# Second layer's projected inputs: half of them moved from attention to the first feed-forward head

## Chip, cores and metric

One core of a Trainium2 chip runs the whole kernel. The metric is the device time of one execution in microseconds; the kernel before is stated as the median of three runs. The trace is of one profiled execution of its own.

## What is computed

The reference is a small encoder of two layers on 768 tokens (two requests of 512 and 256 tokens), width 1024, all in fp32:

```python
for i in range(DEPTH):                                   # DEPTH = 2
    h = rms_norm(x, norm_mix[i])
    x = x + (window_attention(...) if i % 2 == 0 else short_conv(...))
    h = rms_norm(x, norm_mlp[i])
    x = x + jnp.square(jax.nn.relu(h @ mlp_w_up[i])) @ mlp_w_down[i]     # 1024 -> 4096 -> 1024
    gate = jax.nn.sigmoid(rms_norm(x, norm_ple[i]) @ ple_w_gate[i])
    x = x + (p[i] @ ple_w_proj[i]) * gate                # p[i]: 768 x 256
return rms_norm(x, final_norm)
```

The product `p[1] @ ple_w_proj[1]` does not depend on x. It may be computed at any time before the last line of layer 1, and it is this product of which a half moves.

## The kernel before

Activations lie with features on the 128 partitions and the 768 tokens along the free axis: eight blocks `x(m)` of 128 features. A matmul of one block of weights (128 x 128) covers 384 tokens at a time, or 512 and 256 in the attention. Each fp32 product is made of three matmuls: `split` (L81) writes an operand as a high part (a copy on ACT) and a low part (a subtraction on DVE), and high x high, low x high and high x low are summed in PSUM (`group2` L123, `group` L131). `weight` (L92) fetches a block of weights by DMA (SP's queue) and splits it; so each weight costs ACT about one row and DVE another.

The feed-forward part (`mlp`, L853) has 4 groups of 2 "up" chunks and 2 "down" halves for each layer. An up chunk is done in one of two ways. `up_plain` (L897) makes the product directly, in four rounds of 24 matmuls (96 in all). `up` (L956) uses a scheme of seven products instead of eight (`Weights7`, `product7` L434), 84 matmuls in all; it needs sums of activation blocks and sums of weight blocks. The first chunks of a layer are plain, since the sums of activations are made beside them: `Norm7.combine(m)` (L301) makes them on ACT and DVE in a series of pieces (`q` L303, L304 and L320 to L326, `t` L330 and L336). `PLAIN = 3, 2` (L825) says that three chunks are plain in layer 0 and two in layer 1.

The norm before an up chunk is applied after its product: `sum_squares` (L210) adds squares over partitions by four matmuls with ones (`ss`, L226), `acc_parts` (L205) splits their operand (`ah`, `al`), and `rstd_steps` (L234) makes 1/rms on ACT (a table load, two `ln`, one `y`, one `ln`; L242 to L251) and DVE (L252, L259). In `up_plain`, a first chunk for which 1/rms is unknown does `acc_parts` behind its second round and the sum of squares and `rstd_steps` behind its fourth.

PSUM has eight banks: four named A, two B, two C (L103); a product of 768 tokens takes two. Instructions in `mlp` stand in the order in which the code emits them, on ACT, PE and DVE (a manual schedule, L1082); `weave` (L827) takes steps of several lists in turn. In the attention and in its output projection a scheduler sets the order.

`mixer_attention` (L446) handles four groups of heads. Beside some steps of a group it puts other work (`beside`, L778): `inputs1` (L766) loads and splits p[1] in group 0, and `projected(q)` (L759) makes four blocks each of the projected inputs in group 1. `step` (L486) does one block: 12 matmuls (`mm<-p`), copies to `pjs` (L497) and a DMA to DRAM (L498). Scores are matmuls `S` (L667, L668), followed by DVE's row L669 and exponentials on ACT; `queries` (L579) makes the next queries (`mm<-xs_mix`).

Behind the attention, the output projection's loop goes over the eight blocks in the order `PAIRED`, adds the result to `xa` and squares for the norm; `behind(i)` of `first_chunk` (L834) fetches and splits the first up chunk's weights beside it. `mlp` of layer 0 follows.

Of the kernel before, what the change touches and what calls it, by code (L numbers as in the profile page):

```python
# [11 lines left out]
F32 = mybir.dt.float32  # L12
# [6 lines left out]
P = 128  # L19
# [9 lines left out]
CH = 1024  # L29
# [18 lines left out]
def trunk_kernel(ctx: ExitStack, tc: tile.TileContext, a: dict, out: bass.AP):  # L48
# [40 lines left out]
        nc.sync.dma_start(raw[:, : src.shape[1]], src)  # L89
        return raw  # L90

    def weight(src, n, raw=None):  # L92

        m = CH if src is None else src.shape[1]
        if raw is None:
            raw = fetch(src)
        hi = wp.tile([P, CH], F32R, name="whi", bufs=2)
        lo = wp.tile([P, CH], F32R, name="wlo", bufs=2)
        split(hi[:, :m], lo[:, :m], raw[:, :m])
        return blocks(hi[:, :m], n), blocks(lo[:, :m], n)  # L100

# [344 lines left out]
    def mixer_attention():  # L446
# [36 lines left out]
                yield ps[:, :n], o, o + n  # L483
                o += n

        def step(i, w, part, tag, vector):  # L486

            l, m = i // KB, i % KB
            if tag == "L":
                t = ap.tile([P, T], F32, tag="L", name="pjs", bufs=BL)  # L490
            else:
                t = big("pjs")
            for ps, o, e in products(terms_of(w, part, col=m % 4 * P)):
                if vector:
                    dve.tensor_copy(t[:, o:e], ps)
                else:
                    act.activation(t[:, o:e], ps, AF.Copy)  # L497
            nc.sync.dma_start(pj[l][m], t[:])  # L498

        with tc.manual_schedule(engines=order):  # L500
# [31 lines left out]
            w0 = blocks(hi[:], 2), blocks(lo[:], 2)  # L532
            w1 = weight(None, 2, raw=w1)
            for i in range(KB):
                step(i, (w0, w1)[i // 4], part0, "L", i % 2)
# [13 lines left out]
        with s1:  # L549
# [224 lines left out]
            def begin_output():  # L774
# [75 lines left out]

    ET = mybir.EngineType

    def mlp(l, norm, nxt, w, places, early):  # L853


        xs = norm.xs
# [40 lines left out]
        def up_plain(u, w, make, then):  # L897

            nonlocal r

            ps = [both(f"p{i + 1}", {0: "AA", 1: "BC"}.get(u, "AA")[i]) for i in range(2)]
            y1 = y2 = None

            def rects(*which):
# [2 lines left out]


            order = [(0, (0, 6), (0, 1)), (1, (0, 6), (0, 1)), (0, (6, 8), (0, 1)), (1, (6, 8), (0, 1))]
            if u > 0:  # L910
                order = [(i, (0, 8), (o,)) for o in (1, 0) for i in range(2)]
            for n, (i, ks, sides) in enumerate(order):
                for k in range(*ks):
                    m, h = PAIRED[k] % (KB // 2), PAIRED[k] // (KB // 2)
                    c = slice(P * m, P * m + P)
                    hi, lo = w.w[f"w{i + 1}{h + 1}"]
                    for j, (wt, part) in enumerate(((hi, 0), (hi, 1), (lo, 0))):
                        for o in sides:
                            pe.matmul(
                                ps[i][o],  # L920
                                lhsT=wt[:, c],
                                rhs=xs[f"x{h + 1}{1 + o}"][m][part],
                                start=k == 0 and j == 0,
                                stop=k == KB - 1 and j == 2,
                            )
                if n == 0:
                    v = make()
                    split2 = [lambda: v.split("second")] if v.plain else []
                    todo1 = norm.combine(todo.pop(0)) if todo else []
                    rest, pend[:] = pend[:4], pend[4:]  # L930
                    weave(rest, todo1, split2)
                elif n == 1:
                    if r is None:
                        parts = norm.acc_parts()
                    sums = [] if v.plain else [v.sums32, v.sums14, lambda: v.split("direct")]
                    weave(norm.combine(todo.pop(0)) if todo else [], sums, pend)
                    pend.clear()
                elif n == 2:
                    v.split("direct" if v.plain else "s32")
                    if u > 0:  # L940
                        y1, y2 = big("y1"), big("y2")
                        rects((0, 1), (1, 1))
                else:
                    if r is None:
                        steps = norm.rstd_steps(psum, norm.sum_squares(psum, parts=parts, tag="C"))
                        weave(steps, norm.combine(todo.pop(0)) if len(todo) > 1 else [])
                        r = norm.r
                        y1, y2 = big("y1"), big("y2")
                        rects((0, 1), (1, 1))
                    rects((0, 0))  # L950
                    squared(y1)
                    rects((1, 0))
                    pend.extend(acts_of(u, y1, y2, y2))
            return v

        def up(u, w, make, then):  # L956

            w.low("s32")
            w.split("s14")
# [7 lines left out]
            act.activation(c, a, AF.Copy)  # L967
            late()
            w.split("w22")
            late()  # L970
            b = bank("B", "b")[:, :H]
            product7(b, w, "s3", xs, True)
            p = big("p")[:, :H]
            act.activation(p, b, AF.Copy)
# [101 lines left out]
                        add(m, ps[i])  # L1076
                        nxt.block(m, x(m))

        jobs = [(up_plain, 0), (up_plain, 1)]
        for g in range(NG - 1):  # L1080
            jobs += [(up if 2 * g + 2 >= PLAIN[l] else up_plain, 2 * g + 2), (down, g, 0), (down, g, 1), (up, 2 * g + 3)]
# [149 lines left out]

    xs0 = [*range(32, 42), *range(8, 15), *range(16, 20), *range(7)]
    act0 = [7, *range(20, 24), 28, 29, *range(24, 28), 15, 30, 31]

    held = xs0[17:] + act0 + [xs0[16]]
# [2 lines left out]


    n1 = Norm7(2, "mlp0", xs0, act0[7:11], act0[11])
    w0, behind = first_chunk(0, n1, 0)
    w = [weight(a["w_o0"][2], 4), weight(a["w_o2"], 2)]
    for i, m in enumerate(PAIRED):
        if i == 4:
            w[0] = weight(a["w_o0"][3], 4)
        ps = both()
        if m < KB // 2:
            group2(ps, terms_of(w[0], [p[4:] for p in aos], col=m % 2 * P))  # L1250
        else:
            group2(ps, terms_of(w[1], [p[6:] for p in aos], col=(m - 4) * P))
        add(m, ps, xa[m])
        n1.block(m, x(m))
        behind(i)
    n2 = Norm(4, "ple0", xs0[:16], xs0[16])
    mlp(0, n1, n2, w0[0], act0, 0)
    n3 = Norm(1, "mix1", xs0[17:] + act0[:5], act0[5])
    ple(n2, n3, act0[6:9])

# [91 lines left out]
```

## Time and profile before

| | |
|---|---|
| runs | 1717.53, 1717.26, 1715.05 us; median 1717.26 |
| profiled execution | 1715.87 us, its span 1714.1 us |
| busy share of the span | PE 98%, DVE 78%, ACT 50%, POOL 0% |
| matmuls | 9554 |
| DMA | 143.80 MB, mean 84 GB/s |
| attention's end, start of the output projection's loop | 285.2 us |
| loop's end, start of layer 0's chunk 0 | 310.2 us |
| largest single wait of PE in a feed-forward part | 8.0 us, at 344.8 us |

A row of the timeline reads: start, duration, engine, line, operation, output<-inputs, shape, count; in brackets the idle time of the engine ahead of it and who ended it. A row of a wait list reads: engine, its tile and line, what it waited for, then the sum, the number of times and the longest. PE's rows overlap, since matmuls are pipelined; the pace is read from start to start.

### The profile page before, as it was taken

What the parts mean: (1) busy time and instruction counts of PE and PEld (TensorE: products, weight loads), DVE (VectorE), ACT (ScalarE), POOL (GpSimd) and SP (SyncE); (2) the same over time, 40 slices, a digit from 0 to 9 for tenths busy, and PEclk for the clock granted to TensorE, in tenths of its full rate; (3) what the DMA queues carried; (4) which work ended last, traced back from release to release, by engine and by line L of the source; (5) the groups of instructions that cost most, each with busy time, mean ns of one, the idle gap of its engine ahead of it and who ended that gap; (6) DMA issues with size and microseconds to landing.
All of it is one profiled execution on the core that took longest, in us unless ns stands there. A gap on an engine that the chain in (4) does not pass through costs nothing. (4 is left out here: it accounts for less than half of the span.)

```text
span 1714.1 us, 24208 instructions
## 1 busy us (share of the span) xinstructions
PE 1672.0 (98%) x9554; PEld 1616.8 (94%) x9554; DVE 1339.6 (78%) x2198; ACT 855.7 (50%) x1363; POOL 2.0 (0%) x30
## 2 busy tenths in 40 slices
PE   8999999979999999999999999999999999999996
PEld 7887878979999999999999999999999999999986
DVE  7587788878999999977764444667989999999676
ACT  6467756645455455545541111445455555545454
POOL 0000000000000000000000000000000000000000
PEclk9999999989999999999999999999999999999998
DMA  8653331112221222122312121211221222222222
GB/s 263 189 146 110 114 109 62 45 50 74 65 84 62 75 74 74 62 84 93 108 62 62 62 62 62 76 60 49 74 73 64 74 75 74 65 71 86 74 89 96
DMA packets 47554, 143.80 MB, mean 84 GB/s; under 512 B 6048, under 2 KB 10656, under 8 KB 47440
## 3 DMA queue, kind: packets, MB, share of 16 engines
q1 hardware_dynamic: 44880, 139.10, 25.8%
q10 hardware_dynamic: 2560, 3.15, 0.7%
q8 instruction: 75, 1.23, 0.3%
q14 instruction: 39, 0.32, 0.1%
HBM read 122.31 MB, written 10.48 MB: 77 GB/s over the span
## 5 line engine op out<-in xcount | busy, mean ns | idle before, releaser
L83 ACT ACTIVATE whi<-wraw 128x1024 fp32r<-128x1024 f32 (+2 forms) x74 | 76.6, 1035 | 183.9 <-PE b L129 53.2
L409 ACT ACTIVATE whi<-sum 128x1024 fp32r<-128x1024 f32 x55 | 57.9, 1053 | 146.6 <-PE a L441 146.6
L866 ACT ACTIVATE y<-y 128x768 f32<-128x768 f32 x64 | 53.4, 838 | 140.5 <-DVE y L863 140.5
L84 DVE TENSOR_TENSOR wlo<-wraw,whi 128x1024 fp32r<-128x1024 f32 (+2 forms) x74 | 88.2, 1191 | 11.7 <-ACT whi L83 11.4
L441 PE MATMUL a<-act,whi 128*128 128x384 f32 x448 | 96.7, 337 | 0.0
L441 PE MATMUL a<-t,zhi 128*128 128x384 f32 x440 | 90.7, 337 | 1.8 <-ACT c L967 1.8
L441 PE MATMUL b<-t,zhi 128*128 128x384 f32 x440 | 90.5, 337 | 0.9 <-DVE y L863 0.9
L441 PE MATMUL a<-t,whi 128*128 128x384 f32 x440 | 90.5, 337 | 0.0
L1023 DVE TENSOR_TENSOR x<-x,a 128x384 f32<-128x384 f32 x112 | 60.8, 553 | 35.1 <-PE a L441 34.8
L441 PE MATMUL a<-xs,whi 128*128 128x384 f32 x432 | 84.5, 337 | 0.0
L138 PE MATMUL mm<-xs_mix,whi 128*128 128x512 f32 (+1 forms) x320 | 83.3, 342 | 0.0
L441 PEld LDWEIGHTS a<-t,zhi 128*128 128x128 f32 x440 | 77.9, 188 | 2.1 <-ACT c L967 2.1
L441 PEld LDWEIGHTS a<-act,whi 128*128 128x128 f32 x448 | 79.8, 188 | 0.0
L441 PEld LDWEIGHTS b<-t,zhi 128*128 128x128 f32 x440 | 77.7, 188 | 1.2 <-issue 1.2
L441 PEld LDWEIGHTS a<-t,whi 128*128 128x128 f32 x440 | 77.8, 188 | 0.0
L441 PEld LDWEIGHTS a<-xs,whi 128*128 128x128 f32 x432 | 76.3, 188 | 0.0
L420 DVE TENSOR_TENSOR wlo<-wraw,whi 128x1024 fp32r<-128x1024 f32 x60 | 73.0, 1217 | 1.9 <-ACT whi L409 1.9
L420 DVE TENSOR_TENSOR wlo<-sum,whi 128x1024 fp32r<-128x1024 f32 x55 | 67.2, 1222 | 9.2 <-ACT whi L409 9.2
L409 ACT ACTIVATE whi<-wraw 128x1024 fp32r<-128x1024 f32 x60 | 63.2, 1054 | 17.4 <-issue 10.3
L420 DVE TENSOR_TENSOR zlo<-sum,zhi 128x1024 fp32r<-128x1024 f32 x55 | 66.9, 1217 | 1.9 <-ACT zhi L409 1.9
L409 ACT ACTIVATE zhi<-sum 128x1024 fp32r<-128x1024 f32 x55 | 58.3, 1060 | 19.9 <-DVE sum L385 16.1
L330 ACT ACTIVATE t<-y 128x768 fp32r<-128x768 f32 x56 | 47.0, 841 | 40.6 <-DVE y L321 27.9
(279 smaller groups left out, 4647.9 us busy)
## 6 DMA issues: line engine op xcount, KB each, us to landing
wraw<-in_up SPq DMA_DIRECT2D x64, 512.0 KB, 3.5
wraw<-in_down SPq DMA_DIRECT2D x64, 512.0 KB, 3.5
wraw<-in_w_in SPq DMA_DIRECT2D x24, 512.0 KB, 3.4
wraw<-in_gate SPq DMA_DIRECT2D x16, 512.0 KB, 3.5
pj<-pjs SPq DMA_DIRECT2D x16, 384.0 KB, 2.9
wraw<-in_w_q SPq DMA_DIRECT2D x8, 512.0 KB, 4.9
wraw<-in_w_out SPq DMA_DIRECT2D x8, 512.0 KB, 3.4
x_in<-in_x SPq DMA_DIRECT2D x8, 384.0 KB, 7.2
```

What stands on the lines that cost most here:

```text
L83: first = act.activation(hi, src, AF.Copy)
L84: dve.tensor_tensor(lo, src, hi.bitcast(F32), ALU.subtract)
L138: pe.matmul(ps[:, o:e], lhsT=w, rhs=x[:, o:e], start=i == 0 and j == 0, stop=i == n - 1 and j == 2,)
L330: act.activation(t[0][:], (self.q1, self.q2)[i][:], AF.Copy)
L409: act.activation(hi[:], src, AF.Copy)
L420: dve.tensor_tensor(lo[:], src, hi[:].bitcast(F32), ALU.subtract)
L441: pe.matmul(ps, lhsT=a, rhs=b, start=start and i == 0, stop=i == len(terms) - 1, skip_group_check=True)
L866: act.activation(t[:], t[:], AF.Square)
L1023: dve.tensor_tensor(t[:, o : o + H], t[:, o : o + H], f, op)
```

## The change

Four things change. In the attention, `projected` makes four blocks instead of eight. The other four are made by `ahead`, at the head of layer 0's feed-forward part, ahead of chunk 0; for this `second_inputs` loads and splits p[1] and the weights again beside the output projection's loop, where it takes the place of `first_chunk`. In layer 0, two chunks instead of three are plain, so chunk 2 is made by `up`. And the sum of squares and `rstd_steps` stand earlier: in layer 0 in `ahead`, behind the four products; in layer 1 behind chunk 0's second and third rounds. Besides, the first `up` of each layer takes other banks for `c` and `b` and another order of pending work, and `w_o2` lies in other buffers.

```diff
-            def projected(q):
-                w = weight(a["proj"][1, q], 2)
-                for i in range(4):
-                    step(KB + 4 * q + i, w, part1, "t", False)
+            def projected():
+                w = weight(a["proj"][1, 0], 2)
+                for m in range(KB // 2):
+                    step(1, m, w, part1, "t", False)
...
-                (1, 5): (lambda: projected(0), lambda: projected(1)),
+                (1, 5): (projected,),
...
-    PLAIN = 3, 2
+    PLAIN = 2, 2
...
+    def second_inputs(places):
...
+        def behind(i):
+            if i < 2:
+                raw = fetch(a["p"][1, :, i, :])
+                hi, lo = (slot(places[2 * i + p], "p1") for p in range(2))
+                split(hi[:], lo[:], raw[:, :T])
...
+            elif i == 3:
+                ws.append(weight(a["proj"][1, 1], 2))
+            elif i == 5:
+                ws.append(up_chunk(0, 0))
+            elif i == 7:
+                ws[1].split("second")
+
+        def product(m):
+            ps = both("pj", "AB"[m % 2])
+            group2(ps, terms_of(ws[0], part, col=m * P))
+            return ps
...
+    def ahead(norm, product, w, places):
...
+        def copied(m):
+            t = slot(places[m], "pjs", F32)
+            for f, o, e in pieces(ps[m]):
+                act.activation(t[:, o:e], f, AF.Copy)
+            nc.sync.dma_start(pj[1][KB // 2 + m], t[:])
+
+        for m in range(KB // 2):
+            ps.append(product(m))
+            if m == 0:
+                w.split("direct")
+                parts = norm.acc_parts()
+            else:
+                copied(m - 1)
+            if m == 2:
+                weave(norm.combine(0))
+        ss = norm.sum_squares(psum, parts=parts, tag="C")
+        copied(m)
+        weave(norm.rstd_steps(psum, ss), norm.combine(1))
+        return norm.r
...
     def up_plain(u, w, make, then):
...
                 if n == 0:
...
+                    if not known:
+                        parts = norm.acc_parts()
                     weave(rest, todo1, split2)
                 elif n == 1:
-                    if r is None:
-                        parts = norm.acc_parts()
...
+                    if not known:
+                        ss = norm.sum_squares(psum, parts=parts, tag="C")
                 elif n == 2:
-                    v.split("direct" if v.plain else "s32")
+                    weave([lambda: v.split("direct" if v.plain else "s32")], [] if known else norm.rstd_steps(psum, ss))
...
     def up(u, w, make, then):
+            first = u == PLAIN[l]
...
-            late()
-            c = bank("C", "c")[:, :H]
+            if not first:
+                late()
+            c = bank("A" if first else "C", "c")[:, :H]
             act.activation(c, a, AF.Copy)
-            late()
+            late(3 if first else 1)
...
-            b = bank("B", "b")[:, :H]
+            b = bank("A" if first else "B", "b")[:, :H]
...
+            if product:
+                r = ahead(norm, product, w, places[5:7] + places[12:])
+                todo = todo[2:]
...
-    w0, behind = first_chunk(0, n1, 0)
-    w = [weight(a["w_o0"][2], 4), weight(a["w_o2"], 2)]
+    behind, product, w0 = second_inputs(xs0[24:])
+    w = [weight(a["w_o0"][2], 4)] * 2
+    w2 = weight(a["w_o2"], 2, tag="z")
```

On PE, in the attention's second group, these rows stand in before between one S of 384 columns and the next (`mm<-p` are the products that move; four blocks of them follow one another here, with one S pair ahead, and the listing shows the last):

```order
L138 MATMUL mm<-p_1302,whi 128x512
L138 MATMUL mm<-p_1303,whi 128x512
L138 MATMUL mm<-p_1302,wlo 128x512
L138 MATMUL mm<-p_1302,whi 128x256
L138 MATMUL mm<-p_1303,whi 128x256
L138 MATMUL mm<-p_1302,wlo 128x256
L667 MATMUL S<-khh,q 128x384
L668 MATMUL S<-kll,q 128x384
```

And in after at the same place, between the same two S (`mm<-xs_mix` are the next queries; 29 such rows stand there, of which the first and the last are shown):

```order
L666 MATMUL S<-khh,q 128x384
L667 MATMUL S<-kll,q 128x384
L138 MATMUL mm<-xs_mix_166,whi 128x512
L138 MATMUL mm<-xs_mix_165,wlo 128x512
...
L138 MATMUL mm<-xs_mix_186,whi 128x256
L138 MATMUL mm<-xs_mix_187,whi 128x256
L138 MATMUL mm<-xs_mix_186,wlo 128x256
L666 MATMUL S<-khh,q 128x384
L667 MATMUL S<-kll,q 128x384
```

The products are gone, and the next queries, which in before stood among the scores behind, have come forward in their place.

On ACT, at the head of layer 0's feed-forward part, before has this behind the split `ah` of the norm's squares (`zhi` in the sixth row is the high part of chunk 1's weights; `q` and `t` are the pieces of `combine`):

```order
L83 ACTIVATE ah<-acc_mlp_3406 128x768
L303 ACTIVATE q<-x,vec 128x768
L304 ACTIVATE q<-x,vec 128x768
L330 ACTIVATE t_3788<-q 128x768
L330 ACTIVATE t_3793<-q 128x768
L409 ACTIVATE zhi<-wraw 128x1024
L303 ACTIVATE q<-x,vec 128x768
L304 ACTIVATE q<-x,vec 128x768
L242 ACT_TABLE_LOAD
L246 ACTIVATE ln<-ss,eps 128x384 x2
```

After has, from the same row on:

```order
L83 ACTIVATE ah<-acc_mlp_3328 128x768
L887 ACTIVATE pjs<-pj 128x384 x4
L303 ACTIVATE q<-x,vec 128x768
L304 ACTIVATE q<-x,vec 128x768
L330 ACTIVATE t_3678<-q 128x768
L330 ACTIVATE t_3683<-q 128x768
L887 ACTIVATE pjs<-pj 128x384 x4
L303 ACTIVATE q<-x,vec 128x768
L304 ACTIVATE q<-x,vec 128x768
L242 ACT_TABLE_LOAD
L246 ACTIVATE ln<-ss,eps 128x384 x2
```

Eight copies of the new products have come in, and chunk 1's `zhi` is no longer ahead of the norm's rows: it is the fourteenth row behind the last one shown here, with two `ln` and `y` rows, a weight and three more pairs of `t` pieces ahead of it.

More of the change, by code (lines that the diff above doesn't have):

```diff
@@ L90, in fetch, with weight @@
         return raw
[L92 removed]
+    def weight(src, n, raw=None, tag="w"):
         m = CH if src is None else src.shape[1]
@@ L96, in weight @@
             raw = fetch(src)
-        hi = wp.tile([P, CH], F32R, name="whi", bufs=2)
-        lo = wp.tile([P, CH], F32R, name="wlo", bufs=2)
+        pool, bufs = (wp, 2) if tag == "w" else (more, 1)
+        hi, lo = (pool.tile([P, CH], F32R, tag=f"{tag}{p}", name=f"{tag}{p}", bufs=bufs) for p in ("hi", "lo"))
         split(hi[:, :m], lo[:, :m], raw[:, :m])
@@ L943, in up_plain @@
                 else:
[L944 to L947, printed above, removed]
+                    if not known:
                         y1, y2 = big("y1"), big("y2")
@@ L964, in up @@
             product7(a, w, "w11", xs, True)
-            late()
-            c = bank("C", "c")[:, :H]
+            if not first:
+                late()
+            c = bank("A" if first else "C", "c")[:, :H]
             act.activation(c, a, AF.Copy)
-            late()
+            late(3 if first else 1)
             w.split("w22")
             late()
-            b = bank("B", "b")[:, :H]
+            b = bank("A" if first else "B", "b")[:, :H]
             product7(b, w, "s3", xs, True)
```

36 lines of the change are left out of this document (22 added, 14 removed).

## The prediction

> **What bounds the kernel now.** I read the busy times of the page first, then the waits of the matmul engine, then the places where it waits. TensorE is busy nearly the whole span; ACT half of it.
>
> ```profile
> PE 1672.0 (98%) x9554; PEld 1616.8 (94%) x9554; DVE 1339.6 (78%) x2198; ACT 855.7 (50%) x1363; POOL 2.0 (0%) x30
> ```
>
> So a change gains only by removing matmuls, or by removing one of the few stretches in which PE stands still or runs at a lower clock. Windows of 25 us (start and end; then PE busy and its count, PEld, DVE, ACT, POOL, granted clock) show the one large stretch in the part that the change rewrites.
>
> ```profile
> 300.00:325.00 25.00, 25.00 (x145) 25.00 (x144) 24.02 (x36) 17.67 (x23) 0.00 (x0) 1.00 0.16 56
> 325.00:350.00 25.00, 19.78 (x114) 19.45 (x112) 17.43 (x28) 15.12 (x20) 0.00 (x0) 0.99 0.14 43
> 350.00:375.00 25.00, 20.84 (x104) 20.33 (x105) 19.27 (x28) 10.84 (x14) 0.00 (x0) 0.81 0.13 43
> ```
>
> A full window holds 145 matmuls; the two behind it hold 114 and 104. PE's rows in the first feed-forward head of layer 0 show why. Chunk 0 starts at 310.37, the sum of squares at 327.13, chunk 1 behind it ends at 344.8, then comes the hole.
>
> ```profile
> 310.37 0.34 PE L919 MATMUL p<-xs,zhi 128*128 128x384 f32 x1
> ...
> 327.13 0.34 PE L226 MATMUL ss<-ah,ones 128*128 128x384 f32 x1
> ...
> 344.44 0.34 PE L919 MATMUL p<-xs,wlo 128*128 128x384 f32 x1
> 352.79 1.01 PE L919 MATMUL p<-x,zhi 128*128 128x384 f32 x2 [8.01 <-ACT zhi L409]
> 355.17 0.69 PE L919 MATMUL p<-x,zlo 128*128 128x384 f32 x1 [1.37 <-DVE zlo L420]
> 355.66 0.84 PE L919 MATMUL p<-xs,zhi 128*128 128x384 f32 x2
> ```
>
> Chunk 0's 96 matmuls take 16.76 us, 0.1746 us each. Chunk 2 waits 8.01 us for its first weights (zhi, split by ACT), 1.37 us for their low part, and starts at half the pace: after 355.66 two matmuls take 0.64 us. The granted clock agrees.
>
> ```profile
> 356.00:359.00 3.00, 3.00 (x11) 3.00 (x10) 1.41 (x4) 2.45 (x4) 0.00 (x0) 0.50 0.48 175
> 360.00:361.00 1.00, 1.00 (x8) 1.00 (x7) 0.97 (x3) 0.00 (x0) 0.00 (x0) 1.00 0.00 0
> ```
>
> The slow matmuls cost about 2.3 us more (13 between 355.17 and 359.50 take 4.33 us instead of 2.27; the two at 352.79 the rest). ACT's rows say why zhi is late: it is the last of a queue that starts with the norm.
>
> ```profile
> 328.04 0.94 ACT L303 ACTIVATE q<-x,vec 128x768 f32<-128x768 f32 x1 [1.87 <-PE ss L226]
> ...
> 329.82 1.28 ACT L242 ACT_TABLE_LOAD   x1
> 331.12 1.05 ACT L246 ACTIVATE ln<-ss,eps 128x384 f32<-128x384 f32 x2
> ...
> 337.01 0.85 ACT L330 ACTIVATE t<-q 128x768 fp32r<-128x768 f32 x1 [2.34 <-DVE q L326]
> ...
> 351.70 1.04 ACT L409 ACTIVATE zhi<-wraw 128x1024 fp32r<-128x1024 f32 x1
> ```
>
> ACT and DVE hand the pieces of each `combine` to and fro; the hole is a chain between these two engines, not a missing matmul.
>
> **The change, part by part.** All terms are against this execution, 1715.87 us.
>
> *Attention loses four blocks of products.* Here is the stretch that goes (PE, then DVE).
>
> ```profile
> 172.83 0.63 PE L138 MATMUL mm<-p,whi 128*128 128x512 f32 x2
> ...
> 182.07 0.28 PE L138 MATMUL mm<-p,wlo 128*128 128x256 f32 x1
> 182.19 0.34 PE L667 MATMUL S<-khh,q 128*128 128x384 f32 x1
> ```
> ```profile
> 176.59 1.23 DVE L84 TENSOR_TENSOR wlo<-wraw,whi 128x1024 fp32r<-128x1024 f32 x1 [3.75 <-ACT whi L83]
> ...
> 182.75 0.62 DVE L669 CUSTOM_DVE_ANT_0 L<-S,bias,sink 128x384 f32<-128x384 f32 x1 [2.85 <-PE S L668]
> ```
> ```profile
> 172.50:182.75 10.25, 10.20 (x56) 8.71 (x57) 3.14 (x12) 6.74 (x18) 0.00 (x0) 1.00 0.73 266
> 182.75:226.00 43.25, 40.82 (x239) 34.43 (x238) 39.53 (x115) 31.68 (x80) 0.00 (x0) 1.00 0.40 114
> 226.00:285.20 59.20, 58.57 (x350) 50.10 (x349) 49.73 (x143) 36.96 (x93) 0.00 (x0) 1.00 0.17 53
> ```
>
> From 172.83 to 182.19 PE does these products, 9.36 us, with one S pair of 0.34 between them: 9.0 us is the most that can go. But the order of after does not put the next scores (S) there. It puts 29 matmuls of the next queries, 23 of 512 columns and 6 of 256. The products were 24 of each width, so 9.0 us make 0.25 and 0.125 us a matmul and 6.5 us for these 29; and they need their weights split first, on ACT and DVE, as the weights of the products did (wlo ends at 177.8 now). So the next scores come at about 182, as before. Behind that, from 182.75 to 226.00, DVE is busy 39.53 of 43.25 us: PE has 6.5 us less to do there, DVE only one weight split of 1.23 less. At most 3.7 + 1.2 = 4.9 us can go in that stretch; half of its idle time and half of the split would be 2.5. Against this stands that 182 may become 183, as the order puts more ahead of the weight split's low part than now. I take -2.0 us; bounds 0 (DVE sets the pace throughout) and -9.0 (all of it comes through).
>
> *Out-projection loop.* The loop now carries two splits of p, a projection weight and both halves of chunk 0's weights. A low part of p is one DVE row of 128x768 like this one, and one of them stands ahead of the last xa sum, for which PE waits already:
>
> ```profile
> 285.22 0.94 PE L129 MATMUL mm<-aos,whi 128*128 128x384 f32 x4 [0.60 <-DVE xa L736]
> ```
> ```profile
> 325.25 0.96 DVE L336 TENSOR_TENSOR t<-q,t 128x768 fp32r<-128x768 f32 x1
> ```
>
> So the loop starts between 0 and 0.96 us later; +0.3. Inside the loop PE is saturated and DVE has 24.02 of 25 us in the window from 300, part of it chunk work that moves behind the loop, so I cost the rest at nothing; if a split falls between two `add`s, it costs its 1.2 us once. SP gets two fetches of p more, the projection weight later, and four writes of pj among chunk 1's loads. Such a write lands in 2.9 us, and the DMA engines' share in the windows above is 0.16 and less, so these too cost nothing; if a chunk's load were held up by all four, it would land some 12 us later.
>
> ```profile
> pj<-pjs SPq DMA_DIRECT2D x16, 384.0 KB, 2.9
> ```
>
> *The head of layer 0.* Matmuls: 48 of the four products come in, and chunk 2 has 84 instead of 96: +36 x 0.1746 = +6.3 us. The stalls I get by walking the rows of ACT, DVE and PE in the new order, each starting when its engine is free and its inputs are there, with the durations of this trace; the same walk over the old order sets chunk 2's zhi 0.9 us too late, which I take off. The new rows, eight PSUM copies on ACT, have a near relative:
>
> ```profile
> L1018 ACT ACTIVATE B<-a 128x384 f32<-128x384 f32 x56 | 26.9, 481 | 24.7 <-PE a L441 24.7
> ```
>
> Three products run at 310.2 to 316.5. The fourth needs product 1's banks, whose copies stand on ACT behind a zhi and three 128x768 rows (about 3.4 us from 313.1 on by the rows above, and the last, `ah`, waits 1.4 us for DVE's sum): the copies end at 319.5, so PE waits **3.1 us** there (2.4 to 3.1). The sum of squares follows at 321.7, chunk 0 from 322.4 to 339.1. On ACT stand now ahead of chunk 1's zhi the eight copies (3.3 us, as the next one starts before the last has ended), eight q (6.7) and eight t pieces (6.0), the table load (1.3), the `ln` and `y` rows (2.8) and a weight (1.0). The walk's posts are: first q and t pieces done at 323.8, last copies 325.4, table load 328.3, second `ln` 331.1, next t pieces 334.8 (a wait of 2.2 for DVE among them), weight 337.4, t pieces 340.5 (a wait of 1.6), the last ones 344.8. There zhi of chunk 1 starts, less the 0.9 at 343.9. PE therefore waits about **5.8 us** before chunk 1 and **0.9 us** for zlo, then 2.2 us at half clock as now. Chunk 2 finds its weights there. Its end comes at 378.3 - 0.9 + 2.2 = 379.6 against 373.7 now: **+5.9 us**. The other way round: +6.3 of matmuls, while the stalls are 3.1 + 5.8 + 0.9 + 2.2 = 12.0 instead of 8.0 + 1.4 + 2.3 = 11.7. The norm's sums come early, yet its chain still stands behind the new copies, so the hole moves from chunk 2 to chunk 1 and hardly shrinks. Bounds: +3.7 (full clock after the shorter hole) and +8.1 (half clock also behind the fourth product).
>
> After the 8.01 us hole the clock stood at 0.50, while the 1.82 us wait at 1185.62 (below) is followed by a full-rate pace (8 matmuls in 1.67 us): between these two the trace says nothing. [...]
>
> *Layer 1.* Its chunk 2 now writes c and b through bank A and pops the pending work in another order.
>
> ```profile
> 1181.44 1.65 PE L441 MATMUL b<-t,zhi 128*128 128x384 f32 x8 [0.91 <-DVE y L863]
> 1182.93 0.87 PE L441 MATMUL b<-t,zlo 128*128 128x384 f32 x4
> 1185.62 1.67 PE L441 MATMUL a<-t,zhi 128*128 128x384 f32 x8 [1.82 <-ACT c L967]
> ```
>
> Copy c moves ahead of two ACT rows, and up to 0.91 + 1.82 = 2.7 us could go; but DVE's chain, which is unchanged, gives the low part for the next `down` where PE waits already, and takes it back. The norm is summed a round sooner, but ACT's zhi behind it still waits for PE's round 2. I take -0.2; bounds 0 and -2.7.
>
> **Sum:** -2.0 + 0.3 + 5.9 - 0.2 = +4.0, so 1719.9 for this execution. That one is 1.4 us below the median of the runs shown (1717.26), so the forecast at the median's level is **1721.3 us**, +0.23%. A difference under 0.2% (3.4 us) is about what a measurement of this kernel cannot tell from none.
>
> **Rivals.**
>
> *Nearly nothing.* The hole before chunk 1 is 2 us shorter, with the full clock back sooner, or attention gives 4: the sum falls to 0 to +3, some 1717 to 1720.6. For it: every bound above reaches there. Against it: both have to go beyond their nearest rows.
>
> *The hole is filled (faster).* The products' 8.4 us of matmuls stand in the hole's place, so that only issue counts. Then the head costs +6.3 - 8.0 + 3.1 less the slow clock of 2.3, about -0.9, and attention gives 2 to 5: 1711 to 1714. It decides at one point: chunk 1's zhi must start by 339, when chunk 0 ends. For it: sums of squares are out 5.4 us sooner (321.7 against 327.13). Against it: the ACT rows listed above, with the 3.4 us ahead of them, are 24.5 us from 313.1 on; alone they end at 337.6, and any hand-overs of over 1.4 us put zhi past the point. The same result comes from attention alone if its next scores arrive 8 us sooner, against which the order's 29 matmuls speak.
>
> *Twice half clock (slower still).* The clock falls also behind the fourth product's wait, if 3 us are long enough for it, or a smaller PE load in attention leaves gaps as at 158 to 161. That gives +2.2, and with attention at 0 another +2: 1723.5 to 1725.5.
>
> ```profile
> 158.00:161.00 3.00, 2.63 (x10) 2.25 (x11) 2.33 (x7) 0.93 (x3) 0.00 (x0) 0.54 1.04 257
> ```
>
> Here a clock of 0.54 stands beside a PE that is busy for 2.63 of 3 us.
>
> *The change doesn't do what it says* would be that the moved products bring no relief to attention; that is the lower price of 0 above, 1723.3 us.
>
> **How the numbers follow.** Forecast (1719.5 to 1723, moved hole, small attention gain): 0.46. Nearly nothing: 0.22. Filled or full attention gain: 0.14. Slower still: 0.18. Eight times in ten the time lies between 1712 and 1725.5, which takes in half of the faster case and the whole of the slowest. Faster by over 0.2% (below 1713.8): 0.14. Slower by over 0.2% (above 1720.7): 0.18 and 0.36 of the forecast, 0.54 together. Within: 0.22 and the 0.10 of the forecast below 1720.7, 0.32.
>
> **What would show it.** In the changed kernel: a wait of 2.4 to 3.1 us at the fourth `pj` product for the copies of L887; a wait of 5 to 7 us of chunk 1's first matmul for ACT's zhi, with a clock near 0.5 behind it; no wait of over 1 us at chunk 2; 48 more matmuls behind the loop; in attention, scores at 182 and the loop's start about 2 us sooner than 285.2. I am wrong if chunk 1 starts within 2 us of chunk 0's end, if the loop starts 5 us sooner, or if the clock stays at 1.00 throughout the head.

## The result and the profile after

The changed kernel takes 1717.88 us (median of 20 runs, 1715.01 to 1720.30), the kernel before in the same series 1716.99 us (20 runs, 1713.98 to 1719.18). The ratio is 1.0007, with a 95% interval of 1.0000 to 1.0014: +1.2 us, from 0 to +2.4. That is within 0.2%. The forecast was +4.0 us, or 1721.3. The time lies inside its wide range (1712 to 1725.5) but below its main case (1719.5 to 1723), and the outcome held likeliest (slower by over 0.2%) did not come.

The profiled executions differ more: 1720.30 us for after (span 1718.5) against 1715.87 for before. A pair of single executions is thus read with care below: the trace says in which place time goes, the medians say how much in all.

The page's row of busy times of after hardly differs:

```profile
PE 1675.4 (97%) x9542; PEld 1617.8 (94%) x9542; DVE 1346.7 (78%) x2207; ACT 860.1 (50%) x1370; POOL 2.0 (0%) x30
```

Windows of 25 us over the head of layer 0, after:

```profile
300.00:325.00 25.00, 22.72 (x121) 22.21 (x120) 21.87 (x32) 18.39 (x29) 0.00 (x0) 0.93 0.29 96
325.00:350.00 25.00, 19.15 (x99) 18.32 (x98) 18.16 (x27) 17.02 (x22) 0.00 (x0) 0.86 0.17 53
350.00:375.00 25.00, 25.00 (x146) 25.00 (x145) 20.07 (x30) 12.65 (x17) 0.00 (x0) 1.00 0.13 43
```

The empty place has moved: the third window is full now (146 matmuls, 104 before), and the first two have lost 24 and 15. PE's timeline of after shows the two holes:

```profile
308.60 0.86 PE L129 MATMUL pj<-p,whi 128*128 128x384 f32 x4
...
317.35 1.71 PE L129 MATMUL pj<-p,whi 128*128 128x384 f32 x4 [2.28 <-ACT pjs L887]
318.85 0.84 PE L129 MATMUL pj<-p,wlo 128*128 128x384 f32 x2
...
321.25 0.33 PE L226 MATMUL ss<-ah,ones 128*128 128x384 f32 x1
...
344.48 1.01 PE L971 MATMUL p<-x,zhi 128*128 128x384 f32 x2 [5.60 <-ACT zhi L409]
345.74 0.69 PE L971 MATMUL p<-x,zlo 128*128 128x384 f32 x1 [0.25 <-DVE zlo L420]
...
378.12 0.86 PE L441 MATMUL a<-act,whi 128*128 128x384 f32 x4
```

The fourth product waits 2.28 us for the copies of L887, chunk 1 waits 5.60 us for ACT's zhi, and chunk 2 waits for nothing. Behind both waits the clock is at about half, as the granted clock (the third number from the right) of windows over the two places shows:

```profile
317.30:321.20 3.90, 3.85 (x12) 3.66 (x13) 2.34 (x5) 2.87 (x5) 0.00 (x0) 0.56 0.96 297
...
344.40:349.00 4.60, 4.27 (x14) 3.76 (x15) 3.15 (x6) 1.91 (x4) 0.00 (x0) 0.57 0.39 112
349.00:352.00 3.00, 3.00 (x19) 3.00 (x18) 2.61 (x5) 0.91 (x3) 0.00 (x0) 1.00 0.02 8
```

From the first row to `down` the head takes 378.12 - 308.60 = 69.52 us, before 373.72 - 310.37 = 63.35: +6.2 us. From `down` to the end both spans have 1340.4 us left, so layer 1 gave nothing in sum. Its chunk 2 still waits for the copy c, 1.87 us instead of 1.82. The wait of 0.91 us for DVE's `y` ahead of it is gone, but a wait of 0.84 us for another `y` has come behind it:

```profile
1188.76 1.67 PE L441 MATMUL a<-t,zhi 128*128 128x384 f32 x8 [1.87 <-ACT c L1023]
...
1198.26 1.68 PE L441 MATMUL a<-xs,whi 128*128 128x384 f32 x8 [0.84 <-DVE y L1046]
```

**Where the attention's gain shows.** The row of scores ahead of the removed products stands in before and in after at the following times; all PE rows ahead of it are the same in both kernels (first fence before, second after).

```profile
172.49 0.38 PE L667 MATMUL S<-khh,q 128*128 128x256 f32 x1
```
```profile
175.50 0.39 PE L666 MATMUL S<-khh,q 128*128 128x256 f32 x1
175.72 0.28 PE L667 MATMUL S<-kll,q 128*128 128x256 f32 x1
175.84 0.40 PE L138 MATMUL mm<-xs_mix,whi 128*128 128x512 f32 x1
176.07 0.34 PE L666 MATMUL S<-khh,q 128*128 128x384 f32 x1
...
182.49 0.34 PE L666 MATMUL S<-khh,q 128*128 128x384 f32 x1
...
283.45 0.93 PE L129 MATMUL mm<-aos,whi 128*128 128x384 f32 x4 [1.20 <-DVE xa L735]
```

This execution came to the row 3.0 us later than before's, for reasons that lie ahead of the change, and to the output projection's loop 1.8 us sooner (283.45 against 285.22). The part between has therefore lost 4.8 us. The runs below repeat this: 14 traces hold the old or the new attention.

| stretch of PE | old order (5 traces) | new order (8 traces) |
|---|---|---|
| start of the row S 128x256 | 170.2 to 173.4 | 170.2 to 175.5 |
| from it to the second S 128x384 (182.19 in before) | 9.68 to 9.72 | 6.97 to 7.00 |
| from there to the loop's start | 103.0 to 103.7, mean 103.2 | 100.6 to 101.7, mean 101.1 |

The first stretch is 2.7 us shorter, the second 2.1: 4.8 us, with the loop's later start (a wait of 1.20 instead of 0.60 us) already in it. The fourteenth trace is that of the first experiment, e1_attn_half: 172.3, 7.00 and 100.0 us, and its loop starts behind a wait of 0.60 us, as in before.

### The profile page after: what moved, and what is told of

It reads as the page before. It is cut to its first block, busy times and chain, and to the rows that moved or that the text cites. A ratio compares the mean times of both kernels' runs of the same rounds, so it can differ in the third digit from the quotient of the medians.

```text
span 1718.5 us, 24204 instructions
## 1 busy us (share of the span) xinstructions
PE 1675.4 (97%) x9542; PEld 1617.8 (94%) x9542; DVE 1346.7 (78%) x2207; ACT 860.1 (50%) x1370; POOL 2.0 (0%) x30
```

## Experiments

Each was timed in five rounds beside the kernel before on the same chip; the ratio is to that kernel. "Head" is PE's time from the first row behind the output projection's loop to the first `down` row. Two experiments can be told apart when they differ by more than about 2 us.

| kernel | ratio (95%) | us | head, us | PE's waits over 0.4 us in the head |
|---|---|---|---|---|
| before | 1 | 0 | 63.35 | 8.01 zhi, 1.37 zlo |
| after | 1.0007 (1.0000 to 1.0014) | +1.2 | 69.52 | 2.28 copies, 5.60 zhi |
| e1_attn_half | 0.9975 (0.9965 to 0.9985) | -4.3 | 62.66 | 8.01 zhi, 1.38 zlo |
| e2_head_only | 1.0040 (1.0026 to 1.0053) | +6.9 | 70.38 | 2.27 copies, 7.07 zhi |
| e3_plain3 | 1.0019 (1.0010 to 1.0029) | +3.3 | 71.94 | 2.28 copies, 5.53 zhi |
| e4_zhi_early | 0.9991 (0.9983 to 1.0000) | -1.5 | 68.35 | 2.28 copies, 0.50 zlo, 2.63 c |
| e5_copies_first | 0.9986 (0.9977 to 0.9994) | -2.4 | 65.65 | 1.18 zhi, 0.64 zlo, 0.50 zlo, 2.63 c |
| e7_copies_only | 0.9998 (0.9989 to 1.0007) | -0.3 | 69.17 | 8.09 zhi |
| e8_c_first | 0.9987 (0.9978 to 0.9995) | -2.2 | 65.77 | 1.19 zhi, 0.64 zlo, 1.07 d, 1.85 y |
| e10_pool | 1.0001 (0.9992 to 1.0010) | +0.2 | 68.47 | 1.19 zhi, 0.64 zlo, 3.75 whi, 0.66 c, 0.85 y |
| e12_nosums | 0.9979 (0.9971 to 0.9988) | -3.6 | 64.65 | 1.19 zhi, 0.64 zlo, 2.63 c, 0.86 y |
| e6_before_zhi | 0.9990 (0.9982 to 0.9999) | -1.7 | 60.01 | 1.84 zhi, 0.64 zlo, 5.81 y |
| e9_before_zhi_pool | 1.0011 (1.0000 to 1.0021) | +1.9 | 63.58 | 1.83 zhi, 0.64 zlo, 7.87 y |
| e11_before_zhi_nosums | 0.9986 (0.9978 to 0.9995) | -2.4 | 59.47 | 1.83 zhi, 0.64 zlo, 5.28 y |

The us column is the ratio's distance from 1 times 1716. The heads are of one execution each: those of after and e2_head_only, which are the same code, differ by 0.9 us, so a smaller difference says nothing. In the last three kernels the head ends at a wait, and the slow matmuls behind it are not in the column: from `down` to the end they have 1342.1, 1343.8 and 1342.2 us left, all others 1339.7 to 1340.9.

### The two halves apart

Half of the attention's products left out of before, and made nowhere:

```diff
-                (1, 5): (lambda: projected(0), lambda: projected(1)),
+                (1, 5): (lambda: projected(0),),
...
-        nc.sync.dma_start(pr[:, :n], pj[l][m, :, o : o + n])
+        nc.sync.dma_start(pr[:, :n], pj[l][m % 4 if l else m, :, o : o + n])
```

> The kernel before with four of the eight blocks of the second layer's projected inputs left out of the attention, and made nowhere (the last step reads the first four blocks twice). It prices the relief of the attention alone. Theory A (the two traces, aligned row by row around the change: after runs 3.0 us later ahead of the removed products and 1.8 us sooner behind them): -4.8 us, 1712. Theory B (the prediction's term: DVE sets the pace behind): -2.0 us, 1715. If nothing came through: 1717.

-4.3 us, from -6.0 to -2.6: theory A's 4.8 lies inside, the prediction's 2.0 does not. Theory A's figure has the later start of the loop in it, which this kernel doesn't have; without it (0.6) the figure is 5.4 and lies inside as well.

The new head with the old attention:

```diff
-            def projected():
-                w = weight(a["proj"][1, 0], 2)
-                for m in range(KB // 2):
-                    step(1, m, w, part1, "t", False)
+            def projected(q):
+                w = weight(a["proj"][1, q], 2)
+                for i in range(4):
+                    step(1, 4 * q + i, w, part1, "t", False)
...
-                (1, 5): (projected,),
+                (1, 5): (lambda: projected(0), lambda: projected(1)),
```

> The changed kernel, but with all eight blocks still made in the attention as before; four of them are then made a second time in the head, and written over the first. It prices everything except the attention's relief. Theory A: head +6.2, layer 1 nothing, start of the loop +0.6 by the longer wait for the last xa sum: +6 to +7, 1723 to 1724. Theory B (attention gives 2, so that the rest costs 3): 1720.

+6.9 us (4.5 to 9.1), as theory A has it. Of these the head holds 7.0 (70.38 against 63.35); the wait at the loop's start is 1.19 us here and 0.60 in before, which prices that step at +0.6. The two halves sum to +2.6, the change itself measured +1.2; the intervals are wider than the difference. PE's timeline of this kernel also answers how its two holes hang together:

```profile
320.11 1.18 PE L129 MATMUL pj<-p,whi 128*128 128x384 f32 x4 [2.27 <-ACT pjs L887]
...
347.24 1.01 PE L971 MATMUL p<-x,zhi 128*128 128x384 f32 x2 [7.07 <-ACT zhi L409]
```

The fourth product waits as in after (2.27 and 2.28 us), but here the pace hardly drops behind it (12 matmuls in 2.42 us, from 320.11 to 322.53, instead of 3.90). Nothing is won by that: chunk 1 starts 35.88 us behind the head's first row in both kernels, and PE waits 7.07 us ahead of it instead of 5.60. ACT sets this start, whatever PE does before it.

### The third plain chunk

```diff
-    PLAIN = 2, 2
+    PLAIN = 3, 2
```

> The changed kernel with three plain chunks in layer 0, as before: chunk 2 has 96 matmuls again instead of 84. If matmuls alone count: +12 x 0.1746 = +2.1 us on after, 1720. If a hole comes back at chunk 2, since a plain chunk wants its weights sooner: +3 to +6. If the cheaper chunk had brought nothing: 1718.

+3.3 us against before, so +2.1 against after (1.0019 - 1.0007, uncertain by about 2 us), as the 12 matmuls alone give. The head is 2.4 us longer, and chunk 2 has no wait in either trace. So the seven-product chunk is a gain of matmuls and costs no wait in this place.

### Is it the order on ACT that makes the hole?

In after, the split of chunk 1's first weights moved ahead of the last pieces of `combine`:

```diff
                     split2 = [lambda: v.split("second")] if v.plain else []
+                    sooner = known and v.plain
+                    if sooner:
+                        split2.append(lambda: v.split("direct"))
...
-                    weave([lambda: v.split("direct" if v.plain else "s32")], [] if known else norm.rstd_steps(psum, ss))
+                    weave([] if sooner else [lambda: v.split("direct" if v.plain else "s32")], [] if known else norm.rstd_steps(psum, ss))
```

> The changed kernel with the split of chunk 1's first weights (zhi on ACT, zlo on DVE) moved ahead of the last three series of pieces of combine. Theory of the order on ACT: zhi runs at 336.5 instead of 343.4, zlo by 338.4, before chunk 0 ends at 338.9; PE's wait of 5.6 us, 0.25 us and the slow matmuls behind it (2 us) go: -6 to -8 us on after, about 1710.5. Rival: the pieces that are now late make chunk 2 wait, or the buffer of the old weights comes free too late, and under 3 us are won: over 1715.

The hole before chunk 1 is gone: chunk 1 follows chunk 0 without a wait. But only 1.2 us of the head went, and 2.7 us of the time against after (uncertain by about 2), where the theory had 6 to 8: the rival won. PE's timeline of this kernel shows the new place, chunk 2:

```profile
354.24 1.58 PE L441 MATMUL a<-xs,whi 128*128 128x384 f32 x8
355.96 0.97 PE L441 MATMUL a<-xs,wlo 128*128 128x384 f32 x4
356.77 1.57 PE L441 MATMUL b<-t,zhi 128*128 128x384 f32 x8
358.84 0.96 PE L441 MATMUL b<-t,zlo 128*128 128x384 f32 x4 [0.50 <-DVE zlo L420]
362.43 2.93 PE L441 MATMUL a<-t,zhi 128*128 128x384 f32 x8 [2.63 <-ACT c L1026]
```

Counted from the head's first row (307.26 here, 308.60 in after), chunk 2 starts at 46.98 us instead of 54.86, 7.9 us sooner. Then it waits for the copy c, and runs at about half the pace behind it (2.93 us for eight matmuls, 1.57 above). ACT's timeline says that c stands behind a square, which waits 5.19 us for DVE:

```profile
360.21 0.84 ACT L917 ACTIVATE y<-y 128x768 f32<-128x768 f32 x1 [5.19 <-DVE y L914]
360.96 1.04 ACT L409 ACTIVATE whi<-sum 128x1024 fp32r<-128x1024 f32 x1
361.91 0.47 ACT L1026 ACTIVATE c<-a 128x384 f32<-128x384 f32 x1
```

The same edit in the kernel before (with `u > 0` in place of `known`, and an `if not sooner:` ahead of the old split), for its chunk 2:

> The kernel before with nothing changed but the place of chunk 2's zhi and zlo: one series of combine and the pieces of chunk 0's result stand behind them now. Theory of the order on ACT: zhi at 345.5 instead of 351.7, zlo by 347.8; PE's 8.0 + 1.4 us shrink to about 2.9 and the clock stays up: -7 to -9 us, 1708. Rival (the pieces moved back come late for the next half, or the buffer comes free too late): within 3 us of before.

-1.7 us (-3.1 to -0.2) instead of -7 to -9: again the rival. PE's three waits:

```profile
344.43 0.62 PE L919 MATMUL p<-x,zhi 128*128 128x384 f32 x2 [1.84 <-ACT zhi L409]
...
345.69 0.45 PE L919 MATMUL p<-x,zlo 128*128 128x384 f32 x1 [0.64 <-DVE zlo L420]
368.19 1.62 PE L441 MATMUL a<-act,whi 128*128 128x384 f32 x4 [5.81 <-DVE y L863]
```

The hole of 8.01 + 1.37 became 1.84 + 0.64, and a hole of 5.81 us opened at the end of the head, where none was. The head is 3.3 us shorter; 1.7 of it is lost again to the slow matmuls behind the new hole (granted clock 0.56 from 368.1 to 372). What ends the head is thus not the zhi alone; DVE's rectified rows `y` end it too, a few us behind.

### Does removing a wait of PE pay by itself?

The copies of the first two new products moved ahead of `ah` on ACT, first on top of e4_zhi_early, then alone on after:

```diff
             if m == 0:
                 w.split("direct")
-                parts = norm.acc_parts()
             else:
                 copied(m - 1)
             if m == 2:
+                parts = norm.acc_parts()
                 weave(norm.combine(0))
```

> The kernel of e4_zhi_early with the copies of the first two new products moved ahead of the split of the norm's squares (ah) on ACT. The fourth product's wait of 2.3 us and the slow matmuls behind it (1 to 2 us) go in any case. Theory of ACT's queue: ACT's rows up to chunk 1's zhi do not start sooner for it, so that PE waits again ahead of chunk 1 for what it wins: 0 to -1.5 us on e4, 1713 to 1714.5. Rival (waits of PE add up): -3.3 to -4.3 us, 1710 to 1711.

> The changed kernel with only the copies moved ahead of ah. The wait of 2.3 us at the fourth product goes. Theory of ACT's queue: the wait ahead of chunk 1 grows by as much, within 1 us of after (1717). Rival (waits add up): -2.3 to -4 us, 1713 to 1715.

In the second the wait of 2.28 us at the fourth product is gone, and PE's timeline shows where most of it went:

```profile
340.19 1.01 PE L971 MATMUL p<-x,zhi 128*128 128x384 f32 x2 [8.09 <-ACT zhi L409]
```

Before chunk 1 PE waits 8.09 us now instead of 5.60. Yet the theory that ACT's rows do not come sooner isn't quite right either. On ACT `ah` starts 6.57 us behind the head's first row in after and here, since it waits for DVE's sum; the 1.64 us of copies now lie in ACT's idle time ahead of it, and chunk 1 starts at 34.24 us instead of 35.88. So 1.6 us of the gain stay. The head of this trace is only 0.35 us shorter, because the slow pace lasts longer behind the hole: three matmuls take 0.96 us there, from 341.93 up to the row at 346.73, and 0.53 behind it; it lasts 6.7 us instead of 3.9. The time is 1.5 us less than after's by the two ratios, whose intervals overlap; it decides for neither theory.

On top of e4_zhi_early the same edit gives -0.9 us by the ratios, uncertain by about 2 us, which leaves the theory of ACT's queue (0 to -1.5) and speaks against waits that add up (-3.3 to -4.3). The heads of the two traces differ by 2.7; the slow clock behind the fourth product, which took 3.61 us for its 12 matmuls in e4_zhi_early instead of 2.1, is in this. e5_copies_first has the lowest ratio of the kernels that compute everything, 2.4 us under before (1.0 to 3.9).

### Is the next stop the copy c, or DVE's queue?

First c was moved ahead of the square and of a weight split:

```diff
-                    squared(y1)
+                    if v.plain:
+                        squared(y1)
                     rects((1, 0))
+                    if not v.plain:
+                        pend.append(lambda: squared(y1))
...
             w.low("s32")
-            w.split("s14")
             if not first:
+                w.split("s14")
                 late()
...
             act.activation(c, a, AF.Copy)
+            if first:
+                late()
+                w.split("s14")
             late(3 if first else 1)
```

> The kernel of e5_copies_first with the copy of chunk 2's first product (c) moved ahead of a square of chunk 1 and of a weight split on ACT, for both layers. In e4 PE waited 2.6 us for this copy, then ran at half clock for some 4 us (about 2 to 2.5 us lost), and 1.9 us in layer 1. Theory of ACT's queue: -5 to -6 us on e5, about 1708. Rival (the rows moved back are waited for in its place): under 2 us.

Nothing: -2.2 us against -2.4 without it. The wait for c is gone, and PE waits for other rows:

```profile
362.05 1.67 PE L441 MATMUL a<-t,whi 128*128 128x384 f32 x8 [1.07 <-ACT d L1044]
368.37 2.09 PE L441 MATMUL a<-xs,whi 128*128 128x384 f32 x8 [1.85 <-DVE y L1055]
```

Then DVE's queue was tried, by taking four rows of 0.69 us from it. In two kernels GpSimd makes them:

```diff
             self.plain = plain
+            self.adder = dve
...
-            dve.tensor_tensor(a[:, :512], r1[:, :512], r2[:, :512], ALU.add)
+            self.adder.tensor_tensor(a[:, :512], r1[:, :512], r2[:, :512], ALU.add)
...
+                    if l == 0:
+                        v.adder = nc.gpsimd
                     sums = [] if v.plain else [v.sums32, v.sums14, lambda: v.split("direct")]
```

> The kernel of e6_before_zhi with the four sums of weight blocks for layer 0's first half (4 x 0.69 us on DVE, just ahead of the rows that PE waits for in e6) made on GpSimd. Theory of DVE's queue (what PE gains at the hole it loses behind, since DVE's rows reach the end of the head no sooner): the wait of 5.8 us ahead of the first down half shrinks by about 2.8 us, and 0.7 us of the slow clock with it: 1711 to 1712. Rival (the wait is a chain of hand-overs between ACT and DVE and not the length of DVE's queue, or GpSimd slows DVE): within 1 us of e6 (1714.5).

> The kernel of e5_copies_first with chunk 2's four sums of weight blocks made on GpSimd. Theory of DVE's queue: the rectified rows that ACT's square and the copy c wait for come 2.8 us sooner, PE's wait of 2.6 us for c and about 1.5 us of slow clock behind it go: -3 to -4 us on e5, 1709 to 1710. Rival (hand-overs, or GpSimd slows DVE): within 1 us of e5 (1713.2).

Both became slower than the kernels they start from, by about 3.6 and 2.6 us. GpSimd's and DVE's timelines of the first show why:

```profile
349.97 1.64 POOL L385 TENSOR_TENSOR sum<-wraw 128x512 f32<-128x512 f32 x1 [348.67 <-DVE y L320]
351.58 1.59 POOL L390 TENSOR_TENSOR sum<-wraw 128x512 f32<-128x512 f32 x1
```
```profile
349.93 0.56 DVE L321 TENSOR_TENSOR y<-y,y 128x384 f32<-128x384 f32 x1
350.40 1.63 DVE L325 SCALAR_TENSOR_TENSOR q<-q 128x384 f32<-128x384 f32 x1
352.06 1.52 DVE L326 SCALAR_TENSOR_TENSOR q<-q 128x384 f32<-128x384 f32 x1
353.51 1.65 DVE L325 SCALAR_TENSOR_TENSOR y<-y,y 128x384 f32<-128x384 f32 x1
355.19 1.53 DVE L326 SCALAR_TENSOR_TENSOR y<-y 128x384 f32<-128x384 f32 x1
```

In e6_before_zhi, without GpSimd's rows, the same four DVE rows take 0.55 to 0.56 us each; the first:

```profile
347.95 0.55 DVE L325 SCALAR_TENSOR_TENSOR q<-q 128x384 f32<-128x384 f32 x1
```

While GpSimd runs its four rows (two are shown), they take 1.52 to 1.65 us: the four lose 4.1 us, more than the 2.8 that the sums had cost. In e10_pool four DVE rows beside GpSimd's take 1.46 to 1.65 us as well. So these two say nothing on a shorter queue; they say that a longer one costs. The wait at the end of the head grew from 5.81 to 7.87 us.

So the sums were left out altogether, with the raw weights in their place:

```diff
+                    if l == 0 and not v.plain:
+                        v.s = v.raw
...
             (r1, r2), a = self.raw, self.s[0]
+            if self.s is self.raw:
+                return
```

> The kernel of e6_before_zhi with the four sums of weight blocks for layer 0's first half left out (the raw weights stand in for them), so that DVE loses 4 x 0.69 us and nobody else gets work. Theory of DVE's queue: the wait of 5.8 us ahead of the first down half shrinks to about 3, -2.8 to -3.5 us on e6, 1711 to 1712. Rival (hand-overs set it, not the length of the queue): within 1 us of e6, 1714 to 1715.

> The kernel of e5_copies_first with chunk 2's four sums of weight blocks left out in the same way. Theory of DVE's queue: ACT's square, and the copy c behind it, come 2.8 us sooner, PE's wait of 2.6 us for c and some slow clock behind it go: -2.6 to -4 us on e5, 1709 to 1711. Rival (hand-overs): within 1 us of e5, 1712 to 1714.

The first is 0.7 us faster than e6_before_zhi by the ratios, the second 1.2 us faster than e5_copies_first. With about 2 us of uncertainty the second time does not by itself exclude the 2.6 us at least that the theory of DVE's queue had; the waits do. The wait at the end of the head is 5.28 us instead of 5.81, where 3 was expected, and the wait for c is 2.63 us as before. So the theory of the length of DVE's queue falls, and the hand-overs stay. DVE's timeline of the first:

```profile
363.72 0.56 DVE L326 SCALAR_TENSOR_TENSOR y<-y 128x384 f32<-128x384 f32 x1
366.20 1.23 DVE L424 TENSOR_TENSOR wlo<-wraw,whi 128x1024 fp32r<-128x1024 f32 x1 [1.92 <-ACT whi L413]
...
370.21 1.95 DVE L867 SCALAR_TENSOR_TENSOR y<-p,rstd_mlp 128x384 f32<-128x384 f32 x4
```

Where the sums stood, DVE now idles 1.92 us for a weight of ACT's, which stands there behind the pieces `t` that wait for DVE's row at 363.72. The head got 0.54 us shorter for 2.8 us less work. Which of these hand-overs would have to go first was not tried, nor was a kernel with less work for ACT alone. That the head's end is set by the chain between ACT and DVE, and not by PE's holes or by DVE's load alone, is what these kernels agree on.

## Why the prediction was right and wrong

**What bounds the kernel, and the hole: right.** The hole moved from chunk 2 to chunk 1. Predicted waits were 3.1 us at the fourth product (2.4 to 3.1), 5.8 and 0.9 before chunk 1, none at chunk 2; measured 2.28, 5.60, 0.25 and none.

**The head, +5.9: right in sum (+6.2), by errors that cancel.** The waits came out 1.7 us shorter than priced. The clock fell twice and not once: the 12 matmuls of the fourth product took 321.25 - 317.35 = 3.9 us instead of 2.1. That is the condition of the last rival, though the wait ahead of it was 2.28 us and not the 3 us named there, and no run shows a limit of 3 us. The range of the head included it (+8.1). That the wait before chunk 1 was met so closely (5.60 for 5.8) is luck: with a pace that hardly drops behind the fourth product (12 matmuls in 2.42 us), nearly as the forecast had it, the same head waited 7.07 us (e2_head_only). The walk itself was good: counted from the head's first row it ended the last pieces ahead of zhi at 34.6 us, measured 34.9. The 0.9 us then taken off was the error. And the second way to the sum does not give the first: 6.3 + 12.0 - 11.7 is +6.6 and not +5.9, since the stalls listed for before leave 0.7 us of its head unexplained.

**Attention, -2.0 and +0.3 at the loop's start: the step that failed.** Measured together -4.8 against the -1.7 of the sum, from the two stretches of the table, and e1_attn_half agrees. The step was "so the next scores come at about 182, as before". They came at 182.49 in that trace, but in an execution that was 3.0 us late; against their own neighbours they came 2.7 us sooner. The sign "scores at 182" was thus met by chance. The argument had set the 29 matmuls (6.5 us, measured 6.4 from 176.07 to 182.49) against all of the products, and held them by a weight split at a fixed time. But the first of the four removed blocks stood ahead of the S of 384 columns (172.49 to 174.94 in before, 2.45 us), and only one matmul came in its place: that S now follows 0.57 us behind. And the weights were there: `mm<-xs_mix` at 175.84 waits for nothing. The stretch behind, where DVE is the busier engine (39.25 us of 41.51 in after, PE 38.58), gave 2.7 without the later start of the loop; 2.5 was predicted.

**Layer 1, -0.2: nothing.** The wait for c stayed (1.87 for 1.82 us) though c stands further ahead on ACT; the 0.91 us that went came back as a wait for DVE, as the prediction had argued, though at another row.

**The sum.** +4.0 was forecast; with the measured terms it is -4.8 + 6.2 + 0.0 = +1.4, and the medians give +1.2 (0 to 2.4). The case "nearly nothing" had named this way to it (attention gives 4), at a chance of 0.22.

**The single pair of traces would have agreed with the forecast for the wrong reason:** +4.4 us from span to span is +3.0 from ahead of the change and +1.4 from the change.

## What to carry to other kernels

Price a stretch from which work is removed between two rows that both kernels have, not by the clock time of a row: an instruction that "comes at the same time" in an execution that started late has come sooner. A wait of the busiest engine is worth what the next engine's chain leaves of it: five edits here took waits of 2 to 7 us from PE and gave about 0 to 3 us, since the chain between ACT and DVE reached the end of the same section hardly sooner. Look for the latest row of every engine in a section before paying for a hole in one.

## What the runs showed of the hardware

**The clock can fall behind short waits, and need not.** The same instruction waits 1.85 us in before and 1.86 us in after. Below is its row, then PE's windows of 3.41 us around and behind it (PE busy is the second number, the granted clock the third from the right), of before:

```profile
165.89 0.74 PE L138 MATMUL mm<-p,whi 128*128 128x512 f32 x2 [1.85 <-ACT pjs L497]
```
```profile
161.66:165.08 3.42, 2.38 (x14) 1.85 (x13) 0.74 (x2) 2.09 (x9) 0.00 (x0) 1.00 0.72 253
165.08:168.49 3.41, 2.60 (x16) 2.17 (x17) 2.23 (x8) 2.60 (x7) 0.00 (x0) 1.00 0.41 141
```

And of after:

```profile
167.34 1.14 PE L138 MATMUL mm<-p,whi 128*128 128x512 f32 x2 [1.86 <-ACT pjs L496]
```
```profile
164.04:167.46 3.42, 1.56 (x10) 1.16 (x10) 1.18 (x4) 1.86 (x5) 0.00 (x0) 1.00 0.38 144
167.46:170.87 3.41, 3.41 (x13) 2.92 (x14) 1.33 (x4) 1.42 (x4) 0.00 (x0) 0.50 0.41 144
170.87:174.28 3.41, 3.41 (x19) 2.77 (x17) 1.14 (x3) 1.78 (x4) 0.00 (x0) 1.00 0.10 29
```

Full clock in one execution, half in the other. The windows are not chosen freely. Between the start-up and the end of these two traces, the granted clock changes at 158.25, 161.66, 349.40 and 359.64 us in before, and at 160.63, 164.04, 167.45, 170.87, 215.24, 218.65, 317.64, 321.05, 341.53 and 348.36 in after. In each trace all of these lie whole multiples of 3.41 us apart, and the seven stretches at half clock last 3.41 us (five of them), 6.83 (one, in after) and 10.24 (one, in before). On this grid the wait falls into one window in after, which leaves PE busy for 1.56 us of it, and is cut in two in before. Of the windows of the grid in these two traces, half clock followed all in which the profile shows PE idle for 1.86 us or more, and none with 1.21 or less; between these it went both ways (half behind 1.36 to 1.66 us, full behind the 1.82 at 1185.62 in before). In other pairs, too, equal waits had different paces behind them: at the fourth product the 12 matmuls took 3.90 us behind the 2.28 us in after and 2.42 behind the 2.27 in e2_head_only, and behind the 2.63 us for c eight matmuls took 2.93 us in e4_zhi_early, 2.42 in e5_copies_first (granted clock 0.59 from 358 to 362) and 1.67 in e12_nosums (1.00 over the whole head).

This explains the late execution. Of the 3.01 us by which the row S 128x256 came later in after, 1.36 come from the start-up (the same row stands at 23.64 us in before and at 25.00 in after) and 1.56 from the half clock behind the row above. The two traces have one stretch at half clock (before) and two (after) between the start-up and that row. From the second `S<-khh` row of 128x256 ahead of it to that row pass 16.72 us in before (from 155.77) and 18.37 in after (from 157.13). In three of the experiments they are 15.24 to 15.25 us, and the row stands at 170.2 to 170.7; in the other nine they are 16.68 to 16.84, and it stands at 172.3 to 173.6.

**GpSimd's additions slow DVE.** The four rows of DVE shown above took 0.55 to 0.56 us alone (e6_before_zhi) and 1.52 to 1.65 us beside GpSimd's additions (e9_before_zhi_pool), about as long as each of those (1.48 to 1.64). Whether the additions are slowed too was not measured.
